# RG-LRU's squares in a tile of their own, and a new order of projection in the second half of a hybrid RWKV-7 / HGRN2 / RG-LRU layer

## The chip, the cores and the metric

The kernel runs on one core of a Trainium2 chip. The metric is the device time of one execution in microseconds (us), lower is better. The parts of the core that the text speaks of are TensorE (PE in the profile; its weight loads are listed as PEld), VectorE (DVE), ScalarE (ACT), GpSimd (POOL) and SyncE (SP). Each engine takes its own instructions strictly in order, and waits on semaphores for the others and for DMAs. SP issues the plain loads of weights; POOL issues the loads that accumulate.

## The reference

One layer of a recurrent decoder, all in fp32: 1024 prompt tokens and 8 sample tokens, 1032 columns in all, model width 1024.

```python
xn = rmsnorm(x, norm1_g)
pr, ph, pl = split(xn @ w_in)                    # 1408 + 1536 + 512 columns
pm = pr + mu_shift * (pr_previous_token - pr)
o_r = rwkv7(pm)     # 6 heads: S = S(diag(w) - kk^T (a kk)) + v^T k, per token
o_h = hgrn2(ph)     # 6 heads: S = diag(f) S + (1-f) i^T, o = S^T q, rmsnorm, gate
o_l = rglru(pl)     # 256 channels
x = x + concat(o_r, o_h, o_l) @ w_out
x = x + square(relu(rmsnorm(x) @ mlp_w1)) @ mlp_w2
y = rmsnorm(x)
...
def rglru(pl):
    xb, gate = split(pl)
    xc = conv_b + sum(xpad[:, j:j+T] * conv_w[j] for j in range(4))
    r, i = sigmoid(xc @ wa + ba), sigmoid(xc @ wx + bx)
    log_a = -8 * r * softplus(-lam)
    h = scan(exp(log_a), xc * i * sqrt(-expm1(2 * log_a)))
    return h * gelu(gate)
```

The gelu is the tanh form: it needs the square of the gate, gate * (1 + 0.044715 gate^2).

## The kernel before, in words

Channels lie on the 128 partitions, tokens along the free axis. The tokens go through the recurrent part in two halves, of 512 and of 520 columns. Heads are worked two at a time: RWKV has three pairs (r0, r1, r2 in the table `ORDER`), HGRN2 three (h0, h1, h2), RG-LRU two tiles of 128 channels (l0, l1); w is RWKV's low-rank part.

**Dense work.** A dense matmul in fp32 is done in three terms: weights and activations are split into a high part and a rest (`wh`, `wl`, `xh`, `xl`), and `dense_steps` issues wh*xh, wh*xl and wl*xh for each of 8 blocks of 128 rows, 24 matmuls for a tile of 128 output channels and one chunk of columns (the second half has chunks of 256 and 264 in the projections). `in_proj` does this for a tile of 128 columns of `w_in` (a pair of RWKV has 3 tiles, one of HGRN2 has 4: f, q, i, g; an LRU tile has 2: x and gate). `out_proj` does it for `w_out`, first for half 0 (out0_0 to out7_0, 512 columns each, called out0 to out7 below), then for half 1. It splits the finished columns of `mix` into `mh` (ACT, L1243) and `ml` (DVE, L1244), sums over the eight mix tiles in the order 0, 1, 3, 4, 6, 7, 2, 5, and then `evac` adds the residual (DVE, L1248), squares (ACT, L1254) and accumulates (DVE, L1255). After both come the two MLP products.

**Loads of weights.** `load_w` keeps one buffer for the raw weight and two each for `wh` and `wl`. SP loads the raw weight (L290), ACT rounds it to `wh` (L291). Then, for names in the table SOON, DVE subtracts (L293); for all others ACT writes -wh into `wl` (L295) and POOL issues a DMA that adds the raw weight to it (L296).

**Streams.** Beside the dense work run seven streams, written as generators: RWKV's chain (tiles `ch`, `mv`, `st`), two of its block inverses (`gram`, `xm`, `W`, `Y`), its operands (`pw` and others), its finish (`gate`), HGRN2 (`hg_run`: gram and state matmuls, then `ho`, a norm and the transposes `hoT`; in the second half `hg_sample` after it, with `hso` and `hsq`), and RG-LRU (`lru`). `weave` writes PE's order by hand: it keeps a clock `now` that every matmul advances by a cost from `mm` (L76 is where all matmuls are recorded), and takes the stream that is ready by estimated delays (`yield D23` and so on); the dense work fills what is left. The PE order is fixed by this; the other engines' instructions are ordered by the scheduler, with priorities.

**Buffers that hold the order back.** Projected tiles of HGRN2 and RG-LRU live in eight buffers with the tag `hpm`, those of RWKV in six with the tag `pm`. `take("hpm")` holds the dense work until a buffer is free by the planner's count `free["hpm"]`. A pair of HGRN2 takes four and gives them back at the end of `hg_run`; an LRU tile takes three: `xb`, `gl` (the gate) and `gq` (its square), and gives them back behind the last multiplication of `lru` (L1208). In `lru_proj` `gq` is filled as soon as a chunk of the gate leaves PSUM (ACT, L1142). In `lru` itself `gq` then becomes the argument of the tanh (L1158 to L1160), the gelu (L1161), and after the convolution (`lxc`, L1167 to L1172) the buffer of the input gate and of the multiplier of the scan.

The projection order of the second half is `w0 r0 h0 r1 h1 r2 h2 l0 l1`. The weights are loaded in the same order (`start`, the list `ahead`).

Of the kernel before, what the change touches and what calls it, by code (L numbers as in the profile page):

```python
# [9 lines left out]
F32 = mybir.dt.float32  # L10
F32R = mybir.dt.float32r
I32 = mybir.dt.int32
AF = mybir.ActivationFunctionType
# [4 lines left out]
P = 128  # L18
# [8 lines left out]
HW = HT + NB  # L27
# [13 lines left out]
SOON = tuple(f"in{col}_0" for col in (1152, 1280, 0, 384, 768, 2944, 3200, 1408, 1792, 2176, 2560)) + \  # L41
    ("out0_0", "out1_0") + tuple(f"out{m}_1" for m in range(8)) + tuple(f"w1_{f}" for f in range(4))
PRI = [-100, 0, 0, 300, 300, 300, 100, 300]
ORDER = [[(x[0], int(x[1])) for x in half.split()] for half in ("r0 w0 l0 h0 r1 l1 h1 r2 h2", "w0 r0 h0 r1 h1 r2 h2 l0 l1")]
NFB = FF // (FB * P)

COL_R, COL_K, COL_V, COL_WA, COL_G = 0, 384, 768, 1152, 1280
# [1 line left out]
COL_LX, COL_LG = 2944, 3200  # L49
# [3 lines left out]
def kernel(ctx: ExitStack, tc: tile.TileContext, i, o):  # L53
    nc = tc.nc
    V, S, G, PE = nc.vector, nc.scalar, nc.gpsimd, nc.tensor
    act = S.activation
# [37 lines left out]
    def bank_o(name):  # L94

        while now[0] < o_busy[0]:
            yield o_busy[0] - now[0]
        return ps("o", name)

    def used_o(delay=L_O):  # L100
        o_busy[0] = now[0] + delay

    def ev(key, delay=1.5):
        done[key] = now[0] + delay
# [91 lines left out]
    def vec(name, k, n=1):  # L196
        return vt[:, at[name] + k:at[name] + k + n]
# [123 lines left out]
    hgp = phase0.enter_context(tc.tile_pool(name="hgp", bufs=1, side="right"))  # L321
# [74 lines left out]
    free = {"pm": RPM, "hpm": HPM}  # L396

    def take(tag):

        yield lambda: free[tag] > 0  # L400
        free[tag] -= 1
# [8 lines left out]
    def next_w(ask=True):  # L410

        w = ahead.pop(0)()
        if ask:
            ask_w()
        return w


    rb0 = mix[dict(r=0, h=3, l=6)[ORDER[0][-1][0]] + ORDER[0][-1][1]][:, 0:HT]
    early = {}

    def project(hf, col, c0, n, bank="big"):

        pt = ps(bank, f"in{col}_{hf}_{c0}")
        yield from dense_steps(pt[:, :n], *ws_[0], lambda k: xh[k][:, c0:c0 + n], lambda k: xl[k][:, c0:c0 + n])
        return pt[:, :n]

    def take_out(hf, out, pt):

        if hf == 0:
            V.tensor_tensor(out, pt, rb0, op=ALU.mult)  # L430
        else:
            S.copy(out, pt)
# [3 lines left out]
    def in_proj(hf, col, evac, shift=False):  # L436

        if (hf, col) not in early:
            ws_[0] = next_w()
        for c0, n in HCH[hf]:  # L440
            if shift and c0 + n == HW:
                n += NB
            pt = early.pop((hf, col), None)
            if pt is None:
                pt = yield from project(hf, col, c0, n)
            if hf == 0 and ("rb",) not in done:
                yield ("rb",)
            evac(pt, c0, n)
# [439 lines left out]
    hgin, lruin = {}, {}  # L888

    def hp_tile(name):  # L890
        return hgp.tile([P, HW + 3], F32, tag="hpm", name=name, bufs=HPM)
# [237 lines left out]
    def lru_proj(t, hf):  # L1129
        if hf == 1:  # L1130
            yield ("LRU", t, 0)
        x = []
        for w in ("xb", "gl", "gq"):
            yield from take("hpm")
            x.append(hp_tile(f"l{w}{t}_{hf}"))
        xb, gl, gq = x
        G.tensor_copy(xb[:, 0:3], lcar[:, t, 0:3])
        yield from in_proj(hf, COL_LX + t * P, lambda pt, c0, n: take_out(hf, xb[:, 3 + c0:3 + c0 + n], pt))

        def evac_g(pt, c0, n):  # L1140
            take_out(hf, gl[:, c0:c0 + n], pt)
            act(gq[:, c0:c0 + n], gl[:, c0:c0 + n], AF.Square)  # L1142

        yield from in_proj(hf, COL_LG + t * P, evac_g)
        lruin[t, hf] = x
        ev(("lru", t, hf), 1.5)

    def lru(t, hf):
        yield ("lru", t, hf)
        xb, gl, gq = lruin[t, hf]  # L1150
        n = HT if hf == 0 else HW
        s0 = hf * HT

        def f(ap):
            return ap[:, 0:n]


        V.tensor_scalar(f(gq), f(gq), 0.044715, 1.0, op0=ALU.mult, op1=ALU.add)  # L1158
        V.tensor_tensor(f(gq), f(gq), f(gl), op=ALU.mult)
        act(f(gq), f(gq), AF.Tanh, scale=math.sqrt(2.0 / math.pi))  # L1160
        V.scalar_tensor_tensor(f(gl), f(gq), 1.0, f(gl), op0=ALU.add, op1=ALU.mult)  # L1161

        def cw(j):
            return vec("cw", 2 * j + t)

        xc = hgp.tile([P, HW], F32, tag="xc", name=f"lxc{t}_{hf}", bufs=1)
        V.tensor_scalar(f(xc), xb[:, 3:3 + n], cw(3), vec("cb", t), op0=ALU.mult, op1=ALU.add)  # L1167
        cv = cst[:, t, 0:24].rearrange("p (b j) -> p b j", j=3)
        for j in range(3):
            V.scalar_tensor_tensor(xc[:, 0:HT], xb[:, j:j + HT], cw(j), xc[:, 0:HT], op0=ALU.mult, op1=ALU.add)  # L1170
            if hf == 1:
                V.scalar_tensor_tensor(xc[:, HT:HW], cv[:, :, j], cw(j), xc[:, HT:HW], op0=ALU.mult, op1=ALU.add)  # L1172
        if hf == 0:
            V.tensor_copy(lcar[:, t, 0:3], xb[:, HT:HT + 3])
        else:

            so = small.tile([P, 36], F32, tag="lso", name=f"lso{t}", bufs=1)
            V.tensor_copy(so[:, 9:12], xb[:, HT:HT + 3])
            sv = so[:, 12:36].rearrange("p (b j) -> p b j", j=3)
            V.tensor_copy(sv[:, :, 0:2], cv[:, :, 1:3])  # L1180
            V.tensor_copy(sv[:, :, 2], xb[:, 3 + HT:3 + HW])
        rt, it = xb, gq
        yield D39
        for g, (dst, bias) in enumerate(((rt, hba), (it, hbx))):
            for c0, w in (((0, 512),) if hf == 0 else ((0, 260), (260, 260))):
                pt = yield from bank_o(f"lg{t}_{g}_{hf}_{c0}")
                mm(pt[:, 0:w], lruw[:, 2 * g + t, :], xc[:, c0:c0 + w])
                used_o()
                act(dst[:, c0:c0 + w], pt[:, 0:w], AF.Tanh, bias=bias[:, t:t + 1], scale=0.5)
                yield D40  # L1190

        V.scalar_tensor_tensor(f(xc), f(it), 1.0, f(xc), op0=ALU.add, op1=ALU.mult)
        m = gq
        act(f(m), f(rt), AF.Exp, bias=nsp2[:, t:t + 1], scale=nsp2[:, t:t + 1])
        act(f(rt), f(rt), AF.Tanh, bias=sp2[:, t:t + 1], scale=sp2[:, t:t + 1])
        V.scalar_tensor_tensor(f(m), f(m), 1.0, f(rt), op0=ALU.add, op1=ALU.mult)
        V.tensor_scalar(f(rt), f(m), -1.0, 1.0, op0=ALU.mult, op1=ALU.add)

        V.scalar_tensor_tensor(f(m), f(rt), 1.0, f(m), op0=ALU.add, op1=ALU.mult)
        V.tensor_scalar(f(m), f(m), 1e-12, None, op0=ALU.max)  # L1200
        act(f(m), f(m), AF.Sqrt)
        V.scalar_tensor_tensor(f(m), f(m), 0.5, f(xc), op0=ALU.mult, op1=ALU.mult)
        hs = xc
        V.tensor_tensor_scan(hs[:, 0:HT], rt[:, 0:HT], m[:, 0:HT], 0.0 if hf == 0 else lcar[:, t, 3:4], op0=ALU.mult, op1=ALU.add)
        if hf == 1:
            V.tensor_tensor(hs[:, HT:HW], rt[:, HT:HW], cst[:, t, 24:32], op=ALU.mult)
            V.tensor_tensor(hs[:, HT:HW], hs[:, HT:HW], m[:, HT:HW], op=ALU.add)
        V.scalar_tensor_tensor(mix[6 + t][:, s0:s0 + n], f(gl), 0.5, f(hs), op0=ALU.mult, op1=ALU.mult)  # L1208
        free["hpm"] += 3
        ev(("LRU", t, hf), 14.0)  # L1210
        if hf == 0:
            V.tensor_copy(lcar[:, t, 3:4], hs[:, HT - 1:HT])
            return
        V.tensor_copy(so[:, 0:9], hs[:, HT - 1:HW])
        nc.gpsimd.dma_start(o["lru"][t], so)
# [113 lines left out]
    def cols(group, j):  # L1329

        return [c + j * P for c in dict(w=(COL_WA, COL_G), r=(COL_R, COL_K, COL_V), h=(COL_HF, COL_HQ, COL_HI, COL_HG),
                                        l=(COL_LX, COL_LG))[group]]

    def projections():
        for col, bank in zip((col for group, j in ORDER[0] for col in cols(group, j)), ("big", "big", "o")):
            ws_[0] = next_w()
            early[0, col] = yield from project(0, col, 0, HT, bank)
        for hf in range(2):
            for group, j in ORDER[hf]:
                yield from dict(w=rw_lora, r=rw_proj, h=hg_proj, l=lru_proj)[group](j, hf)  # L1340
# [34 lines left out]
    def start():  # L1375

        ahead.extend((lambda col=col, hf=hf: load_w(i["w_in"][col // P], f"in{col}_{hf}", parts=2 if not hf and col == COL_WA else 1))
                     for hf in range(2) for group, j in ORDER[hf] for col in cols(group, j))
        ahead.extend((lambda m=m, hf=hf: load_w(i["w_out"][m], f"out{m}_{hf}")) for hf in range(2) for m in range(KT))
# [128 lines left out]
    for m in range(KT):  # L1508
        if m < 6:
            tag = ("wh8", "wl8", "raw8", "wl8", "wh8", "last")[m]  # L1510
            w = (mlp if m == 5 else wpool).tile([P, 2, FB, P], F32R, tag=tag, name=f"w2_{m}", bufs=2 if tag[0] == "w" else 1)
# [94 lines left out]
```

## Time and profile before

| | |
|---|---|
| time, median of three runs | 1594.58 us (1592.06 to 1597.8) |
| profiled execution, own time | 1598.09 us |
| its span | 1596.3 us |
| mean granted TensorE clock | 0.973 of full speed |
| PE busy | 1501.6 us, 94% of the span |
| PE weight loads busy | 1323.8 us, 83% |
| DVE busy | 770.7 us, 48% |
| ACT busy | 664.2 us, 42% |
| POOL busy | 382.8 us, 24% |

The own time of an execution is a little longer than its span, which runs from the first to the last recorded instruction. The second half's projections run from about 330 us on, the part that the change reorders lies between about 466 and 791 us, and from 791 us to the end there is only dense work (the rest of out_proj, then the MLP). In the views below, a row of the table by stretches of time gives the length of the stretch, then the busy time of PE, PEld, DVE, ACT and POOL with the number of instructions in brackets, the mean granted clock, the share of the DMA engines and GB/s. A row of the timeline gives start, duration, engine, line, operation and tiles, and in square brackets the wait ahead of it with the one that ended it.

### The profile page before, as it was taken

How to read it: one execution, taken by the hardware profiler on the slowest of the kernel's cores; microseconds unless marked ns; L12 is line 12 of the kernel's file. 1: busy time of each engine (PE TensorE's matmuls, PEld its weight loads, DVE VectorE, ACT ScalarE, POOL GpSimd, SP SyncE). 2: the span in 40 equal slices, each digit the busy share in tenths (PEclk: the TensorE clock that was granted, in tenths of full speed). 3: DMA queues.
4: the chain of work that ended last, by engine and by line, in shares of the span. 5: the costliest groups of instructions: out<-in, count | busy, mean ns of one | idle time of the engine just before them, and what ended most of it. 6: DMA issues, size and time to landing. Idle time of an engine off the chain costs nothing.

```text
span 1596.3 us, 30293 instructions
## 1 busy us (share of the span) xinstructions
PE 1501.6 (94%) x12536; PEld 1323.8 (83%) x12536; DVE 770.7 (48%) x1799; ACT 664.2 (42%) x1435; POOL 382.8 (24%) x531
## 2 busy tenths in 40 slices
PE   8879998998998989888899999999999999999997
PEld 6767776898997888777698989998989998989887
DVE  7778756766466657764465322222222222322224
ACT  4544656546346454454344423233232423233132
POOL 4553224225235245232222010101111010111011
PEclk9999999999899999978899999999999999999999
DMA  4325334334233344204533453535454454544242
GB/s 160 115 68 107 80 76 93 72 81 112 61 82 90 71 103 100 55 29 114 139 110 103 106 92 82 106 80 106 80 106 80 99 100 90 96 88 98 53 94 107
DMA packets 53081, 146.89 MB, mean 92 GB/s; under 512 B 6960, under 2 KB 7248, under 8 KB 52944
## 3 DMA queue, kind: packets, MB, share of 16 engines
q0 software_dynamic: 22976, 65.33, 24.7%
q1 hardware_dynamic: 29824, 79.61, 15.5%
q8 instruction: 98, 1.61, 0.4%
q14 instruction: 39, 0.32, 0.1%
q10 hardware_dynamic: 144, 0.04, 0.0%
HBM read 138.87 MB, written 6.07 MB: 91 GB/s over the span
## 4 chain that ended last, share of the span: by engine, by line
PE 45%; issue 5%; DMA 4%; DVE 3%; ACT 2%; POOL 1%; POOLq 0%; ACTq 0%; DVEq 0%
PE up L76 21%; PE dn L76 20%; PE out L76 2%; DMA raw_out<-in_w_out 1%; DMA wl_out<-in_w_out 1%; DMA wl_w<-in_w 1%; DMA raw_w<-in_w 1%; PE ch L76 1%; ACT wh_out L291 1%; PE in L76 1%; DVE wl_out L293 0%; PE fin L81 0%; DMA w<-in_w 0%; DVE ml L1244 0%; ACT wh_w L291 0%
## 5 line engine op out<-in xcount | busy, mean ns | idle before, releaser
L76 PE MATMUL in<-xl,wh_in 128*128 128x512 f32 (+3 forms) x648 | 222.2, 343 | 1.9 <-DVE xl L385 1.9
L76 PE MATMUL in<-xh,wl_in 128*128 128x512 f32 (+3 forms) x648 | 220.6, 340 | 3.4 <-DMA wl_in<-in_w_in 1.9
L76 PE MATMUL dn<-hh,wl_w 128*128 128x264 f32 (+2 forms) x696 | 222.9, 320 | 0.7 <-DMA wl_w<-in_w 0.6
L76 PE MATMUL dn<-hh,wh_w 128*128 128x264 f32 (+2 forms) x696 | 223.0, 320 | 0.0
L76 PE MATMUL dn<-hl,wh_w 128*128 128x264 f32 (+2 forms) x696 | 222.9, 320 | 0.0
L76 PE MATMUL in<-xh,wh_in 128*128 128x512 f32 (+3 forms) x648 | 221.7, 342 | 0.0
L1494 DVE TENSOR_TENSOR mix<-mix,dn 128x512 f32<-128x512 f32 (+2 forms) x192 | 98.3, 512 | 242.6 <-PE dn L76 242.6
L296 POOL DMA_DIRECT2D wl_w<-in_w x86 | 75.0, 875 | 574.4 <-ACT hh L1424 301.2
L291 ACT ACTIVATE wh_w<-raw_w 128x512 fp32r<-128x512 f32 (+1 forms) x90 | 70.6, 785 | 281.0 <-PE dn L76 228.2
L1423 DVE SCALAR_TENSOR_TENSOR rl<-up,rl 128x512 f32<-128x512 f32 (+2 forms) x96 | 49.5, 516 | 202.2 <-ACT rl L1422 202.2
L76 PE MATMUL up<-nxh,wh_w 128*128 128x264 f32 (+1 forms) x512 | 144.9, 283 | 0.1
L76 PE MATMUL up<-nxl,wh_w 128*128 128x264 f32 (+1 forms) x512 | 144.2, 282 | 0.5 <-POOL nxl L1320 0.5
L76 PE MATMUL up<-nxh,wl_w 128*128 128x264 f32 (+1 forms) x512 | 144.5, 282 | 0.0
L76 PEld LDWEIGHTS dn<-hh,wl_w 128*128 128x128 f32 x696 | 130.9, 188 | 13.6 <-DMA wl_w<-in_w 3.6
L76 PEld LDWEIGHTS dn<-hl,wh_w 128*128 128x128 f32 x696 | 131.0, 188 | 10.1
L76 PEld LDWEIGHTS dn<-hh,wh_w 128*128 128x128 f32 x696 | 131.1, 188 | 9.5
L76 PEld LDWEIGHTS in<-xl,wh_in 128*128 128x128 f32 x648 | 126.5, 195 | 14.6 <-DVE xl L385 4.6
L76 PEld LDWEIGHTS in<-xh,wl_in 128*128 128x128 f32 x648 | 126.3, 195 | 14.1 <-DMA wl_in<-in_w_in 2.4
L76 PEld LDWEIGHTS in<-xh,wh_in 128*128 128x128 f32 x648 | 126.3, 195 | 9.6 <-issue 0.2
L76 PE MATMUL up<-nh,wh_w 128*128 128x512 f32 x256 | 101.6, 397 | 0.0
L76 PE MATMUL up<-nl,wh_w 128*128 128x512 f32 x256 | 101.6, 397 | 0.0
L76 PE MATMUL up<-nh,wl_w 128*128 128x512 f32 x256 | 101.5, 397 | 0.0
(461 smaller groups left out, 3283.6 us busy)
## 6 DMA issues: line engine op xcount, KB each, us to landing
raw_in<-in_w_in SPq DMA_DIRECT2D x53, 512.0 KB, 3.3
wl_in<-in_w_in POOLq DMA_DIRECT2D x43, 512.0 KB, 5.5
raw_w<-in_w SPq DMA_DIRECT2D x32, 512.0 KB, 3.3
raw_w<-in_w SPq DMA_DIRECT2D x64, 256.0 KB, 2.6
wl_w<-in_w POOLq DMA_DIRECT2D x58, 256.0 KB, 4.1
wl_w<-in_w POOLq DMA_DIRECT2D x28, 512.0 KB, 5.5
raw_out<-in_w_out SPq DMA_DIRECT2D x16, 512.0 KB, 3.4
out_y_prompt<-yt SPq DMA_DIRECT2D x16, 256.0 KB, 2.0
```

The lines of the kernel that those rows point to most:

```text
L76: PE.matmul(out, lhsT, rhs, start=start, stop=stop)
L291: act(wh[:, ks], raw[:, ks], AF.Copy)
L296: G.dma_start(wl[:, ks], src[:, ks], accum_op=ALU.add)
L1423: V.scalar_tensor_tensor(rl[:, :n], pt[:, :n], 0.0, rl[:, :n], op0=ALU.max, op1=ALU.mult)
L1494: V.tensor_tensor(x2[m][:, c0:c0 + n], x2[m][:, c0:c0 + n], pt[:, :n], op=ALU.add)
```

## The change

Two things. First, `gq` no longer takes one of the eight shared `hpm` buffers. It is a tile of its own (tag `lq`, one buffer), which is requested when the LRU stream starts; the square moves with it, from two activations in `lru_proj` (one for each chunk of the second half) to one over the whole width in `lru`. An LRU tile so takes two `hpm` buffers and not three. Second, in the second half the projection order changes from `r1 h1 r2 h2` to `r1 r2 h1 h2`: RWKV's third pair is projected directly behind its second.

```diff
-ORDER = [[...] for half in ("r0 w0 l0 h0 r1 l1 h1 r2 h2", "w0 r0 h0 r1 h1 r2 h2 l0 l1")]
+ORDER = [[...] for half in ("r0 w0 l0 h0 r1 l1 h1 r2 h2", "w0 r0 h0 r1 r2 h1 h2 l0 l1")]
...
 def lru_proj(t, hf):
-        for w in ("xb", "gl", "gq"):
+        for w in ("xb", "gl"):
             yield from take("hpm")
             x.append(hp_tile(f"l{w}{t}_{hf}"))
-        xb, gl, gq = x
+        xb, gl = x
...
-        def evac_g(pt, c0, n):
-            take_out(hf, gl[:, c0:c0 + n], pt)
-            act(gq[:, c0:c0 + n], gl[:, c0:c0 + n], AF.Square)
-
-        yield from in_proj(hf, COL_LG + t * P, evac_g)
+        yield from in_proj(hf, COL_LG + t * P, lambda pt, c0, n: take_out(hf, gl[:, c0:c0 + n], pt))
...
 def lru(t, hf):
-        xb, gl, gq = lruin[t, hf]
+        xb, gl = lruin[t, hf]
+        gq = hgp.tile([P, HW], F32, tag="lq", name=f"lq{t}_{hf}", bufs=1)
...
+        act(f(gq), f(gl), AF.Square)
         V.tensor_scalar(f(gq), f(gq), 0.044715, 1.0, op0=ALU.mult, op1=ALU.add)
...
-        free["hpm"] += 3
+        free["hpm"] += 2
```

Every engine's order is the same as before through the whole first half, up to row 1724 of PE (466 us in the trace), and again from PE's row 3059 (the second chunk of half 1's out_proj, 791 us). Only what lies between is reordered. On SP the raw loads of r2's three weights move ahead of those of h1's four, on POOL the accumulating DMAs likewise. On PE the last `gram5` of HGRN2's second pair moves from row 2209 to 2430 and its `hsq` from 2437 to 2555; the first `pw` of RWKV's third pair moves from 2257 to 2039 and its last `gate` from 2998 to 2977. Names in the rows below: `in3200_1_256` is the projection of column 3200 of `w_in`, second half, chunk at 256; 2944 and 3200 are x and gate of l0, 3072 and 3328 those of l1.

PE at the end of l0's projection, before:

```order
L76 MATMUL in3200_1_256_8092<-xh7_3192,wh_in3200_1_7685 128x264
L76 MATMUL in3200_1_256_8092<-xl7_3200,wh_in3200_1_7685 128x264
L76 MATMUL in3200_1_256_8092<-xh7_3192,wl_in3200_1_7686 128x264
L76 MATMUL gram4_2_1_8186<-rq0_196,kq4_2_1_8126 64x2x32 x8
L76 MATMUL W3_2_1_1_8213<-xm_2_1_1_7880,sa_2_1_1_7878 64x64 x8
L76 MATMUL ch_2_1_0_8079<-st0_2_1_0_8167,az_186 128x64
L76 MATMUL Y3_2_1_1_8226<-ym_2_1_1_7879,wm3_2_1_1_8212 64x64 x8
L76 MATMUL ch_2_1_0_8079<-rh1_2_1_0_8224,yz_187 128x64
L76 MATMUL gram5_2_1_8239<-rq1_197,kq5_2_1_8179 64x2x32 x8
```

The same place now:

```order
L76 MATMUL in3200_1_256_8099<-xh7_3192,wh_in3200_1_7961 128x264
L76 MATMUL s_mean2_8146<-s_os2_7953,bones_84 128x8
L76 MATMUL in3200_1_256_8099<-xl7_3200,wh_in3200_1_7961 128x264
L76 MATMUL in3200_1_256_8099<-xh7_3192,wl_in3200_1_7962 128x264
L76 MATMUL in3072_1_0_8163<-xh0_3185,wh_in3072_1_8057 128x256
L76 MATMUL in3072_1_0_8163<-xl0_3193,wh_in3072_1_8057 128x256
L76 MATMUL in3072_1_0_8163<-xh0_3185,wl_in3072_1_8058 128x256
```

Before, 37 rows of stream matmuls (the third HGRN2 pair's `gram`, the inverse's `W` and `Y`, the chain's `ch`) stand between l0's last matmul and l1's first; now none does.

DVE at the end of LRU tile 0 (its last multiplication writes mix6) and the beginning of LRU tile 1 (`lq1`, `lxc1`), now; `mix1<-out1` is the residual addition behind out1:

```order
L728 COPY mv_2_1_1_7469<-ch_2_1_1_8374 128x64
L1205 TENSOR_TENSOR lxc0_1_8185<-lxc0_1_8185,lq0_1_8179 128x8
L1246 TENSOR_TENSOR mix1_70<-out1_0_8614,xr1_0_8612 128x512
L1206 SCALAR_TENSOR_TENSOR mix6_75<-lgl0_1_7958,lxc0_1_8185 128x520
L1212 COPY lso0_8193<-lxc0_1_8185 128x9
L1156 TENSOR_SCALAR lq1_1_8544<-lq1_1_8544 128x520
L1165 TENSOR_SCALAR lxc1_1_8550<-lxb1_1_8153,vt_77 128x520
L1157 TENSOR_TENSOR lq1_1_8544<-lq1_1_8544,lgl1_1_8154 128x520
L1253 TENSOR_TENSOR acc0_8453<-acc0_8453,sq1_0_8662 128x512
```

Before, mix6 stood nine rows ahead of the first operation on lxc1, among operations of the chain and the finish, with no addition of an out tile ahead of either. Now the addition behind out1 stands ahead of mix6, and the second LRU tile's operations follow it directly.

PE at the first gate matmul of LRU tile 1 (`lg1_0_1_0`, which reads lxc1), before:

```order
L76 MATMUL out1_0_8789<-mh7_8683,wl_out1_0_8776 128x512
L76 MATMUL ch_2_1_1_8588<-st1_2_1_1_8767,az_186 128x64
L76 MATMUL out1_0_8789<-mh2_8678,wh_out1_0_8775 128x512
L76 MATMUL out1_0_8789<-ml2_8686,wh_out1_0_8775 128x512
L76 MATMUL lg1_0_1_0_8813<-lxc1_1_8725,lruw_204 128x260
L76 MATMUL out1_0_8789<-mh2_8678,wl_out1_0_8776 128x512
```

And now:

```order
L76 MATMUL out1_0_8614<-ml5_8467,wh_out1_0_8600 128x512
L76 MATMUL out1_0_8614<-mh5_8459,wl_out1_0_8601 128x512
L76 MATMUL out2_0_8674<-mh0_8454,wh_out2_0_8606 128x512
L76 MATMUL out2_0_8674<-ml0_8462,wh_out2_0_8606 128x512
L76 MATMUL lg1_0_1_0_8677<-lxc1_1_8550,lruw_204 128x260
L76 MATMUL ch_2_1_1_8374<-mv_2_1_1_7469,bt_2_1_1_7222 128x64
```

The gate matmul has moved from inside out1 to three rows behind out1's last.

More of the change, by code (lines that the diff above doesn't have):

```diff
@@ L43 @@
 PRI = [-100, 0, 0, 300, 300, 300, 100, 300]
-ORDER = [[(x[0], int(x[1])) for x in half.split()] for half in ("r0 w0 l0 h0 r1 l1 h1 r2 h2", "w0 r0 h0 r1 h1 r2 h2 l0 l1")]
+ORDER = [[(x[0], int(x[1])) for x in half.split()] for half in ("r0 w0 l0 h0 r1 l1 h1 r2 h2", "w0 r0 h0 r1 r2 h1 h2 l0 l1")]
 NFB = FF // (FB * P)
```

## The prediction

> **What bounds the kernel now.** I read the first part of the page for the share of each engine, then the chain of waits by engine, then the table by stretches of time.
>
> ```profile
> PE 1501.6 (94%) x12536; PEld 1323.8 (83%) x12536; DVE 770.7 (48%) x1799; ACT 664.2 (42%) x1435; POOL 382.8 (24%) x531
> PE 45%; issue 5%; DMA 4%; DVE 3%; ACT 2%; POOL 1%; POOLq 0%; ACTq 0%; DVEq 0%
> ```
>
> PE is busy for 94% of the span and leads the chain; no other engine reaches 50%. So a change that leaves PE's work alone can only win where PE idles or where its clock is low. The five stretches show where that is:
>
> ```profile
> 466.00:669.00 203.00, 186.78 (x2432) 168.96 (x2434) 134.54 (x391) 103.26 (x284) 82.85 (x114) 0.99 0.36 83
> 669.00:691.00 22.00, 19.16 (x252) 15.61 (x253) 11.59 (x33) 9.41 (x22) 5.15 (x10) 0.61 0.21 49
> 691.00:737.00 46.00, 37.67 (x261) 32.49 (x261) 25.99 (x63) 21.21 (x59) 13.30 (x16) 0.81 0.20 55
> 737.00:791.00 54.00, 45.34 (x235) 36.14 (x234) 25.47 (x48) 27.56 (x50) 11.59 (x17) 0.94 0.60 151
> 791.00:1596.00 805.00, 786.51 (x5078) 712.38 (x5078) 253.81 (x491) 259.51 (x464) 106.03 (x125) 1.00 0.44 94
> ```
>
> From 466 to 669 us and from 791 us on PE is full at full clock. Between lie 122 us of two defects: PE busy 82 to 87%, and a clock of 0.61, 0.81 and 0.94. The first of the three begins where the dense work stops and ends where it starts again:
>
> ```profile
> 668.68 0.28 PE L76 MATMUL in<-xh,wl_in 128*128 128x264 f32 x1
> 668.89 0.69 PE L76 MATMUL gram<-rq,kq 128*64 128x64 f32 x16
> ...
> 685.45 1.23 PE L76 MATMUL lg<-lxc,lruw 128*128 128x260 f32 x2
> ...
> 690.77 0.36 PE L76 MATMUL in<-xh,wh_in 128*128 128x256 f32 x1
> ```
>
> The last matmul of l0's projection starts at 668.68, the first of l1's at 690.77. This is the hole in front.md's first pair of order rows: h1 and h2 hold all eight `hpm` buffers, and when h1's four come back l0 takes three, so l1 must wait. In the hole only stream matmuls are left, and they run slowly: the pair of `lg` at 685.45 takes 1.23 us, the same pair inside out_proj 0.60 (row below). The clock is what differs:
>
> ```profile
> 680.00:690.00 10.00, 10.00 (x136) 8.06 (x136) 4.47 (x13) 4.30 (x10) 1.73 (x4) 0.50 0.01 3
> 739.18 0.60 PE L76 MATMUL lg<-lxc,lruw 128*128 128x260 f32 x2
> ```
>
> PE counts as busy for 10.00 of 10 us there, at a clock of 0.50, so it does 5 us of work. Busy time times clock gives the work at full clock: 19.16 x 0.61 = 11.7 us, 37.67 x 0.81 = 30.5, 45.34 x 0.94 = 42.6, together 84.8 us in 122 us.
>
> **The change part by part.**
>
> *The hole is filled.* With two buffers for an LRU tile, h1's four serve l0 and l1, and l1's projection follows l0's without a stream row between. The third RWKV pair's chain starts earlier too (its first `pw` moves from PE row 2257 to 2039, the last `gate` from 2998 to 2977), so that the streams run beside dense work and not alone. PE's work is the same. The full stretch (466 to 669) does 186.78 x 0.99 / 203 = 0.91 us of work in each us. At that rate the three stretches need 11.7 / 0.91 = 12.8, 30.5 / 0.91 = 33.5 and 42.6 / 0.91 = 46.8 us: they lose 9.2, 12.5 and 7.2 us, 28.9 in all. I take the first two, 21.7, and leave the 7.2 where they are, since out2 to out7 wait there for weights, whose loading isn't changed:
>
> ```profile
> PE out L76 <- DMA wl_out<-in_w_out: 8.1, 4, 4.4
> PE gate L76 <- DVE mix L782: 2.9, 1, 2.9
> PE hsq L76 <- DVE hssq L1115: 2.2, 1, 2.2
> ```
>
> The first row's 8.1 us are four waits of PE between 690 and 792. The waits for `gate` and `hsq` are of the size that the 9% of the full stretch already holds.
>
> *The end of LRU tile 0 in front of tile 1.* This adds a wait. By front.md's last order rows DVE now has the addition behind out1 (mix1) ahead of mix6, and everything for the second LRU tile behind that; and PE has `lg1_0_1_0`, which needs the finished lxc1, three rows behind out1's last matmul. So from out1's end PE does two matmuls and then waits for a string of DVE instructions. Their groups, each with busy time and mean ns:
>
> ```profile
> L1248 DVE TENSOR_TENSOR mix<-out,xr 128x512 f32<-128x512 f32 x8 | 5.5, 690 | 9.1 <-PE out L76 9.1
> L1255 DVE TENSOR_TENSOR acc<-acc,sq 128x512 f32<-128x512 f32 x7 | 4.8, 688 | 2.7 <-ACT sq L1254 2.7
> L1170 DVE SCALAR_TENSOR_TENSOR lxc<-lxb,vt,lxc 128x512 f32<-128x512 f32 x6 | 4.5, 744 | 0.0
> L1172 DVE SCALAR_TENSOR_TENSOR lxc<-lcst,vt,lxc 128x8 f32<-128x8 f32 x6 | 2.9, 480 | 0.0
> L1159 DVE TENSOR_TENSOR lgq<-lgq,lgl 128x520 f32<-128x520 f32 x2 | 1.4, 696 | 0.0
> L1208 DVE SCALAR_TENSOR_TENSOR mix<-lgl,lxc 128x520 f32<-128x520 f32 x2 | 1.4, 694 | 0.0
> L1161 DVE SCALAR_TENSOR_TENSOR lgl<-lgq,lgl 128x520 f32<-128x520 f32 x2 | 1.4, 680 | 1.8 <-ACT lgq L1160 1.8
> L1167 DVE TENSOR_SCALAR lxc<-lxb,vt 128x520 f32<-128x520 f32 x2 | 1.1, 547 | 0.6 <-ACT lxb L432 0.6
> L1158 DVE TENSOR_SCALAR lgq<-lgq 128x520 f32<-128x520 f32 x2 | 0.9, 427 | 0.7 <-ACT lgq L1142 0.7
> L1178 DVE COPY lso<-lxb 128x3 f32<-128x3 f32 x2 | 0.4, 210 | 0.0
> ```
>
> 0.69 (mix1) + 0.69 (mix6) + 0.43 + 0.55 + 0.70 + 0.69 (acc) + 3 x 0.74 (convolution) + 0.68 (gelu) = 6.7 us. With three of L1172 and four copies it is 6.7 + 7 x 0.21 (L1178's) = 8.1 to 6.7 + 3 x 0.48 + 4 x 0.21 = 9.0. I take the lower end, since one of the six L1172 is far longer than the rest, and take 0.6 for the two matmuls in front: 7.5 us of waiting. Queued behind it on PE are out2 to out7, all dense. A wait of this size also costs clock. The nearest row is a wait of 4.39 us for a weight, with the 10 us around it:
>
> ```profile
> 765.53 0.73 PE L76 MATMUL out<-mh,wl_out 128*128 128x512 f32 x1 [4.39 <-DMA wl_out<-in_w_out]
> 760.00:770.00 10.00, 5.61 (x20) 4.20 (x20) 3.08 (x8) 2.52 (x3) 3.03 (x5) 0.83 0.84 183
> ```
>
> A clock of 0.83 over 10 us loses 1.7 us. Together 9.2 us; at least 0, if out2's weight is what PE would wait for in that time anyway (the 8.1 above are then paid at once).
>
> The Trainium skill, page "TensorE: Matmul & The Clock Gate", Part 1, says that the clock halves after an idle window of about 3.4 us and is full again after about 3.4 us of sustained work. This trace agrees in the size behind the 4.39 us wait, but not in the hole, where PE is busy for 10.00 of 10 us at 0.50. By the rule the `hoT` wait below, past 3.4 us as well, would cost 1.7 us more, and the sum would be a gain of 6.3 us and not 8.0.
>
> *HGRN's second pair moves back.* With r2 projected first, h1's matmuls come later and its tail is squeezed: 125 PE rows from the second pair's last `gram5` to its `hsq`, where there were 228. The step from `ho` to `hoT` is the tight one:
>
> ```profile
> 590.47 1.72 PE L76 MATMUL ho<-hst,rq 128*64 128x64 f32 x32
> 603.35 0.66 PE L81 MATMUL hoT<-ident,hot 128*128 128x128 f32 x4 [2.23 <-DVE hot L1083]
> 572.34 0.69 PE L76 MATMUL gram<-rq,kq 128*64 128x64 f32 x16
> 616.34 0.28 PE L76 MATMUL hsq<-hssq,bones 128*128 128x8 f32 x2
> ```
>
> From 592.2 to 603.35 pass 11.2 us, 2.2 of them idle. In the new order fewer rows stand between: I estimate 3 us more of waiting (between 0 and the 9 that are covered now), and 1.5 for `hso` and `hsq`: 4.5 us.
>
> *The square.* One activation over 520 columns in place of two over 256 and 264, on ACT, which is under half busy. For tile 0 dense work covers it. For tile 1 its buffer comes free ahead of mix1, so it runs while DVE waits for out1: nothing. Without that cover it delays L1158 by its own length, which no row shows at this width; DVE's operations on 520 columns take 0.43 to 0.70 us.
>
> *Loads.* On SP three raw loads of r2, on POOL their accumulating DMAs, pass four of h1, in the order in which PE uses them: nothing. If the cover failed, the price is that of the waits for projection weights now:
>
> ```profile
> PE in L76 <- DMA wl_in<-in_w_in: 1.9, 2, 1.6
> ```
>
> **The sum.** 21.7 - 9.2 - 4.5 = 8.0 us gained. The profiled execution took 1598.1 us, 3.5 above the median of the runs: 1590.1 against it, 1586.6, or 1587, against the median of 1594.58. Bounds: with `lg1`'s clock and HGRN's waits at nothing the gain is 8.0 + 1.7 + 4.5 = 14.2 (1580); with half of the second stretch's 12.5 not recovered, 1.7 (1593).
>
> **The rivals.**
>
> *All of the hole, no new wait.* If DVE has mix1's place early enough, or out2's weight is late anyway, and `hoT` is covered, the gain is 21.7 to 28.9 us: 1566 to 1573. For it: DVE is 48% busy, and the scheduler has let such waits vanish in most places of the full stretch. Against it: the string is in DVE's order, and it can't begin before out1's end. Chance 0.20.
>
> *HGRN's tail is a latency, not a matter of rows (slower).* From `gram5` to `hsq` the second pair took 616.34 - 572.34 = 44.0 us over 228 rows, 0.193 us a row. 125 rows now give 24 us. If the tail needs the 44 whatever stands beside it (DVE, ACT and POOL between), PE waits 20 us in place of the 4.5: 15.5 us more, a loss of 7.5, 1602. It decides against the change from 4.5 + 8.0 = 12.5 us of idle PE in that stretch on. For it: the waits for `hoT` are there even with 228 rows. Against it: the waits for `hoT` and `hsq` are 2.2 us each at most, so much of the 44 us is PE's own queue. Chance 0.17.
>
> *The clock does not come back.* If the small matmuls themselves pull the clock down, the hole's 19.16 us of busy time stay 19.16, not 11.7: the gain shrinks by 7.5 to 0.5 us, 1594. Against it: the same small matmuls run between dense ones at 0.99 from 466 to 669 us. Chance 0.08.
>
> That the change doesn't do what it says is ruled out by the order: l1's first row follows l0's last.
>
> **How the numbers follow.** My forecast has 0.55. A measurement of this kernel can tell 0.3%, 4.8 us. Of the forecast's own range, 1580 to 1593, three quarters lie below 1589.8: 0.41, and 0.14 within. With the first rival faster has 0.61. Same: 0.14 + 0.08 + 0.03 of the second rival, 0.25. Slower: the 0.14 left. The range reaches to 1570, two fifths into the first rival's, and to 1602, the middle of the second's: some 0.12 lies below and 0.08 above.
>
> **What would show it.** In the new profile: no stretch of over 5 us without a dense matmul between 466 and 740 us, and no clock of 0.5 to 0.6 there over 10 us (right), or one (the third rival). A wait of PE `lg` for DVE `lxc` of about 7 us behind out1, with the clock down after it; if it is under 2, the first rival. The waits of `hoT`, `hso` and `hsq` for the second pair summing to about 4.5 us above now; 12 or more and the second rival has it. The waits for `wl_out` at about 8 us as now; if they grow, a loss that I have not priced. The prediction is wrong if the time from PE's row 1724 to row 3059, 325 us now, is not 311 to 323 (the bounds of the sum).

## The result, and the profile after

The changed kernel takes 1580.78 us (median of 20 runs, 1572.17 to 1590.88) against 1594.51 us before (20 runs, 1591.04 to 1602.88): the ratio is 0.9912, 95% interval 0.9895 to 0.9929, a gain of 13.7 us where 7.5 were forecast (1587 against 1594.58). The profiled execution of the changed kernel took 1572.8 us, 8.0 below its median, and that of before 1598.09, 3.5 above. So the two traces differ by 25 us, more than the kernels do, and 3 of the 25 lie ahead of the first moved row (466.08 us before, 463.04 now), where the two programs are the same.

The page after, first the busy times, then the chain of waits by engine:

```profile
PE 1489.7 (95%) x12536; PEld 1312.6 (84%) x12536; DVE 771.2 (49%) x1799; ACT 663.7 (42%) x1433; POOL 382.8 (24%) x531
PE 74%; DVE 11%; ACT 6%; DMA 4%; issue 4%; POOL 1%; POOLq 0%; SPq 0%; ACTq 0%; DVEq 0%
```

PE has the same 12536 matmuls and is 12 us less busy with them (1501.6 before): they are the same, the clock under them is higher. The stretches of time of the changed kernel show where; the reordered part now ends at 766.3 us and not at 791:

```profile
463.00:624.00 161.00, 152.46 (x1997) 139.57 (x1997) 104.61 (x304) 86.68 (x225) 61.17 (x89) 1.00 0.37 84
624.00:646.50 22.50, 18.15 (x299) 14.86 (x298) 13.26 (x41) 9.54 (x46) 11.28 (x16) 0.77 0.30 76
646.50:702.40 55.90, 54.04 (x492) 46.90 (x491) 42.74 (x107) 31.09 (x68) 19.86 (x26) 1.00 0.35 84
702.40:720.00 17.60, 10.79 (x56) 8.95 (x56) 9.06 (x24) 6.84 (x11) 2.69 (x5) 0.81 0.41 97
720.00:766.30 46.30, 41.20 (x337) 32.74 (x335) 27.30 (x58) 25.97 (x63) 17.96 (x21) 1.00 0.60 150
766.30:1571.00 804.70, 786.39 (x5078) 712.10 (x5078) 254.63 (x492) 259.77 (x464) 106.30 (x125) 0.99 0.44 94
```

Busy time times clock adds up to 270.4 us of work from 463 to 766.3, and before to 269.8 (185 + 84.8), so the method counts the same work in both traces. Before it took 325 us, now 303. Two rows stand out, 624 to 646.5 at a clock of 0.77 and 702.4 to 720 with PE busy 10.79 of 17.6 us. PE's timeline has the reasons:

```profile
624.01 0.28 PE L76 MATMUL in<-xh,wl_in 128*128 128x264 f32 x1
...
646.48 0.36 PE L76 MATMUL in<-xh,wh_in 128*128 128x256 f32 x1
...
663.24 0.29 PE L76 MATMUL in<-xh,wl_in 128*128 128x264 f32 x1
663.36 0.28 PE L76 MATMUL in<-xh,wh_in 128*128 128x256 f32 x1
...
709.24 0.80 PE L76 MATMUL lg<-lxc,lruw 128*128 128x260 f32 x1 [6.81 <-DVE lxc L1168]
```

At 663 us l1's projection follows l0's without a gap: the hole that the prediction spoke of is gone. But at 624 there is another, of 22.5 us, that it didn't speak of. Between the last matmul of h2's projection and the first of l0's PE has only stream matmuls. h1 and h2 hold all eight buffers, and the new order brings h1's pair later, so that now l0 and not l1 waits for its end. And at 702.4 begins the wait at `lg` that was forecast. PE's waits from 690 to 767 us, in total, number and longest:

```profile
PE lg L76 <- DVE lxc L1168: 6.8, 1, 6.8
PE ho L76 <- DVE hst L1060: 2.6, 3, 1.2
PE out L76 <- DMA wl_out<-in_w_out: 1.9, 2, 1.3
```

The waits for `wl_out` went from 8.1 us to 1.9. On DVE, the string that ends the wait at `lg`:

```profile
702.29 0.69 DVE L1246 TENSOR_TENSOR mix<-out,xr 128x512 f32<-128x512 f32 x1
702.89 0.69 DVE L1206 SCALAR_TENSOR_TENSOR mix<-lgl,lxc 128x520 f32<-128x520 f32 x1
...
709.10 0.22 DVE L1170 SCALAR_TENSOR_TENSOR lxc<-lcst,vt,lxc 128x8 f32<-128x8 f32 x1
```

From mix1 at 702.29 to the end of lxc1's last operation pass 7.0 us, where the prediction summed 8.1 at the lower end. And mix1 shows no wait ahead of it: DVE came to it as out1 ended (the last matmul ends at 702.44), with work behind work since 688 us.

### The profile page after: what moved, and what is told of

The parts are those of the page before. It is cut to its first block, busy times and chain, and to the rows that moved or that the text cites. A ratio compares the mean times of both kernels' runs of the same rounds, so it can differ in the third digit from the quotient of the medians.

```text
span 1571.0 us, 30303 instructions
## 1 busy us (share of the span) xinstructions
PE 1489.7 (95%) x12536; PEld 1312.6 (84%) x12536; DVE 771.2 (49%) x1799; ACT 663.7 (42%) x1433; POOL 382.8 (24%) x531
## 4 chain that ended last, share of the span: by engine, by line
PE 74%; DVE 11%; ACT 6%; DMA 4%; issue 4%; POOL 1%; POOLq 0%; SPq 0%; ACTq 0%; DVEq 0%
PE up L76 22%; PE dn L76 21%; PE in L76 14%; PE ch L76 3%; PE W L76 2%; PE out L76 2%; PE Y L76 2%; PE gram L76 1%; DMA raw_out<-in_w_out 1%; PE sc L76 1%; DMA raw_w<-in_w 1%; ACT wh_out L291 1%; DMA raw_in<-in_w_in 1%; DVE rq L981 1%; DMA wl_w<-in_w 1%
## 5 line engine op out<-in xcount | busy, mean ns | idle before, releaser
L76 PEld LDWEIGHTS in<-xh,wl_in 128*128 128x128 f32 x648 | 124.7, 192 | 11.7 <-DVE wl_in L293 1.9
L1420 ACT ACTIVATE rl<-up 128x512 f32<-128x512 f32 (+2 forms) x96 | 43.3, 451 | 139.5 <-PE up L76 139.5
```

The source lines that it names most:

```text
L76: PE.matmul(out, lhsT, rhs, start=start, stop=stop)
L1420: act(rl[:, :n], pt[:, :n], AF.Relu)
```

## The experiments

The theory after the result: the gain is the filled hole, and the wait at `lg` and the new hole take part of it back. Two rivals: that the gain comes from the third RWKV pair's earlier chain, and that the waits are paid once, whatever ends them. All times are medians, all ratios are to the kernel before, timed beside the experiment.

**Half of the change: the buffers alone.**

```diff
-... "w0 r0 h0 r1 r2 h1 h2 l0 l1"
+... "w0 r0 h0 r1 h1 r2 h2 l0 l1"
```

> The squares in their own tile and two shared buffers for an LRU tile, with the old projection order (r1 h1 r2 h2). In PE's order l1's projection then follows l0's directly, as in the changed kernel; RWKV's third pair is projected as late as before. Theory A (the gain is the hole in the dense work, and only the buffers close it): nearly the whole gain, 8 to 16 us below the kernel before, and no stretch at clock 0.5 between l0 and l1. Theory B (the gain is that the third RWKV pair's chain starts earlier and ends earlier): within 4 us of the kernel before, since its last gate still comes at PE row 3064.

Measured: 1576.91 us, ratio 0.9900 (0.9874 to 0.9926). The same stretch of time as the hole of before, then the rest of the reordered part:

```profile
669.00:691.00 22.00, 22.00 (x296) 20.18 (x296) 12.75 (x30) 11.25 (x25) 5.18 (x9) 1.00 0.31 73
691.00:776.00 85.00, 73.05 (x472) 59.96 (x472) 51.75 (x117) 46.75 (x105) 25.95 (x34) 0.90 0.50 123
```

From 669 to 691 us PE is busy all the time at full clock, where before it did 11.7 us of work. The buffers alone give as much as the whole change or more (the intervals overlap): theory A holds. The profiled execution was the slowest of the six (1582.58 us).

**The other half: the order alone.**

```diff
-        for w in ("xb", "gl"):
+        for w in ("xb", "gl", "gq"):
```

(and the square back in `lru_proj`.)

> The new projection order with three shared buffers for an LRU tile, as before the change. In PE's order 45 rows of stream matmuls stand again between l0's projection and l1's. Theory A (the hole): 0 to 5 us from the kernel before, with a stretch of some 15 to 20 us at a clock of about 0.5. Theory B (the third RWKV pair earlier): 8 to 16 us below the kernel before.

Measured: 1589.97 us, ratio 0.9979 (0.9961 to 0.9997). The hole ahead of l1 is back, 23 us, and so is the clock of one half:

```profile
664.00:687.00 23.00, 17.80 (x142) 13.74 (x140) 14.92 (x41) 11.55 (x36) 6.62 (x9) 0.63 0.21 46
670.00:680.00 10.00, 8.49 (x67) 6.63 (x63) 6.63 (x16) 4.67 (x22) 1.85 (x2) 0.50 0.25 48
```

The order alone gains some 3 to 6 us (by the ratio and by the medians) with both holes in it, l0's and l1's. So the buffers carry the gain, but the order is not worth nothing.

**The waiting matmul moved.** The gate matmuls of LRU tile 1 come later on PE, behind out2's end; nothing else changes.

```diff
-        yield D39
+        yield D39 + (8 if (t, hf) == (1, 1) else 0)
```

> The changed kernel with 8 us more of estimated delay ahead of LRU tile 1's gate matmuls, so that the first of them stands at PE row 2892 and not 2860, behind out2. Theory A (the wait for lxc1 is a loss by itself): the wait of 6.8 us behind out1 is gone, and with it the lower clock: 6 to 9 us below the changed kernel, about 1572 to 1575. Rival (out2 and out3 wait for their weights in that time anyway, so the wait is paid once whatever ends it): waits for wl_out grow by 4 to 6 us and the time is within 3 us of the changed kernel.

Measured: 1567.41 us, ratio 0.9839 (0.9810 to 0.9868). The changed kernel, timed beside it (below), took 1585.38; a gain of 6 to 9 us on it was expected. PE's largest wait from 690 to 767 us, then the two stretches in which the changed kernel waited:

```profile
PE out L76 <- DMA wl_out<-in_w_out: 5.1, 5, 2.0
```

```profile
700.00:710.00 10.00, 8.97 (x55) 7.13 (x54) 9.10 (x24) 5.40 (x7) 2.87 (x5) 1.00 0.80 180
710.00:720.00 10.00, 9.09 (x113) 7.43 (x112) 3.92 (x13) 7.04 (x25) 2.23 (x3) 1.00 0.58 137
```

The wait is gone, and the waits for weights grow from 1.9 to 5.1, so the rival has some 3 us. From out2's first matmul to the end of the reordered part (766.3 us in the first profile of the changed kernel) pass 57.1 us here, and 64.4, 69.1 and 66.3 us in the three profiles of the changed kernel. The wait at `lg` so cost 7 to 12 us, about the 9.2 of the prediction. By the medians of the two kernels, timed together, it cost 18 us, which is more than the profiles show. This version is faster than both kernels by far.

**The changed kernel again, twice.**

> The changed kernel itself once more, for a second profile: its 20 runs lie between 1572 and 1591 us, and the profiled one was 8 us below their median. If the spread comes from the clock, this profile shows the same waits as the first (lg behind out1 about 6.8 us) and low-clock stretches at other places; if it comes from waits, these differ by several us. The median should be 1578 to 1584.

> The changed kernel a third time. Its two profiles have the same waits of PE to within 1 us, but 5.1 us between them, in the stretch from 730 to 760 us, where one has a granted clock of 1.00 and the other 0.66, 0.96 and 0.87 over three times 10 us. Theory (the spread of this kernel's runs is where and how long the clock stays low behind its waits and behind the hole ahead of l0): again lg about 6.8 us, the hole from 624 to 646 us, and a median of 1579 to 1587. Rival: other waits than in the first two profiles.

Measured: 1585.38 us (12 runs), ratio 0.9939 (0.9917 to 0.9960), and 1582.56 (6 runs), 0.9911 (0.9889 to 0.9933); the first median is just above the 1578 to 1584 that were expected. The wait at `lg` is 6.8 us all three times. What differs is the clock; the same stretch in the first, second and third profile of the changed kernel:

```profile
730.00:740.00 10.00, 8.56 (x50) 6.97 (x49) 6.79 (x21) 4.30 (x19) 7.58 (x9) 1.00 0.34 109
```

```profile
730.00:740.00 10.00, 7.59 (x32) 5.96 (x32) 5.76 (x18) 4.38 (x25) 6.06 (x7) 0.66 0.15 37
```

```profile
730.00:740.00 10.00, 9.36 (x39) 7.55 (x40) 5.09 (x18) 4.40 (x19) 6.63 (x8) 0.67 0.31 85
```

Over all 38 runs the median is 1582.2 us. The fastest 12 average 1577.8 us at a mean clock of 0.979, the slowest 12 average 1587.8 at 0.974. A clock lower by 0.005 over 1580 us would be 8 us of those 10. But a run that waits longer also has a lower mean clock, so the lists alone don't show which comes first. Between the first two profiles it is the clock: their waits are the same to within about 1 us, and from 730 to 760 us the mean clock is 1.00 in the first and 0.83 in the second, which is worth about the 5.1 us between them. All three profiled executions lie well below the medians that go with them (1572.8, 1577.91 and 1577.26 us), so no trace shows what an execution of 1585 us does. That it loses its time by the clock too is likely, and not shown; at which places stays open.

**The wait's buffer.** LRU tile 1's lxc gets a buffer that tile 0 doesn't hold, so that DVE can fill it early; PE's order stays.

```diff
-        xc = hgp.tile([P, HW], F32, tag="xc", name=f"lxc{t}_{hf}", bufs=1)
+        xc = hgp.tile([P, HW], F32, tag="xc" if (t, hf) != (1, 1) else "kq", name=f"lxc{t}_{hf}", bufs=1 if (t, hf) != (1, 1) else 2)
```

> The changed kernel with LRU tile 1's convolution result lxc1 in another buffer (one of the two that HGRN2 uses for kq), so that it need not wait until tile 0 is done with the one xc buffer; PE's order is unchanged, and DVE's puts all of lxc1's operations some 20 rows ahead of the addition behind out1. Theory A (PE waits at lg1 for the end of a string of DVE work that the one buffer ties to tile 0's end): the wait of 6.8 us behind out1 falls below 2 us with PE's order as it is, and the time is 6 to 12 us below the changed kernel, 1570 to 1576. Rival (DVE is full in that stretch, whatever its order): the work moved ahead delays the ml splits and HGRN's operations by as much, new waits of 4 to 7 us stand at gram, ho or out, and the time is within 4 us of the changed kernel.

Measured: 1585.64 us, ratio 0.9911 (0.9883 to 0.9938), so no gain. Rows of PE, ACT and DVE:

```profile
720.48 1.24 PE L76 MATMUL lg<-lxc,lruw 128*128 128x260 f32 x2 [5.29 <-ACT lxb L1187]
```

```profile
719.95 0.48 ACT L1187 ACTIVATE lxb<-lg,hba 128x260 f32<-128x260 f32 x1 [2.45 <-DVE lso L1179]
```

```profile
719.54 0.17 DVE L1176 COPY lso<-lxb 128x3 f32<-128x3 f32 x1 [1.31 <-DMA out_lru<-lso]
```

The first gate matmul no longer waits (it starts at 710.13). But the third waits 5.29 us, for ACT to empty its bank into `lxb`. ACT waits for DVE's copies of `lxb` into `lso`, and these for tile 0's output DMA, since `lso` too has one buffer. The wait went to the next buffer that the two tiles share. The rival's result holds, though the new wait is not at `gram`, `ho` or `out`, where it was expected, and at its end a DMA is waited for, not DVE's work (DVE is idle for the last 1.31 us ahead of the copies). The clock took more as well, in the hole ahead of l0:

```profile
640.00:650.00 10.00, 9.16 (x87) 6.89 (x83) 4.32 (x13) 0.78 (x3) 4.06 (x6) 0.50 0.07 28
650.00:660.00 10.00, 10.00 (x62) 9.71 (x62) 4.23 (x15) 0.48 (x2) 5.07 (x6) 0.54 0.08 26
```

Here the clock stays at half for 9.4 us after the dense matmuls have come back (at 649.9). In the changed kernel's first profile, with the same order on PE, it was full again 4.9 us before they came back (at 646.48). First this run, then the changed kernel's first profile:

```profile
649.90:659.30 9.40, 9.40 (x57) 9.11 (x58) 4.23 (x15) 0.58 (x2) 4.61 (x5) 0.50 0.08 28
```

```profile
631.40:641.60 10.20, 8.68 (x89) 6.64 (x87) 3.87 (x12) 3.33 (x18) 4.32 (x5) 0.50 0.20 56
641.60:646.50 4.90, 3.72 (x75) 3.08 (x75) 3.20 (x10) 0.30 (x2) 3.56 (x5) 1.00 0.15 57
```

So PE's order alone does not fix how long the clock stays down; what does is open.

**Idle matmuls in the old hole.** In the kernel before, 86 matmuls (128x256) of l0's last weight, whose result nobody reads, go into the hole ahead of l1.

```diff
+        if (t, hf) == (1, 1):
+            pt = ps("big", "fill")
+            while free["hpm"] < 3:
+                mm(pt[:, 0:256], ws_[0][0][:, 0, :], xh[0][:, 0:256])
+                yield 0.0
```

> The kernel before with 86 idle matmuls (128x256, l0's last weight times xh, never read) put into the hole between l0's and l1's projection, wherever the planner has nothing else there. They are some 10 us of work at full clock. Theory A (the clock halves there because PE has only small matmuls to do, and dense ones bring it back): the hole keeps its length of about 22 us or grows by up to 3, with a clock near 1.0, and the time is within 4 us of the kernel before in spite of the 10 us of work. Rival (the small matmuls themselves take that long): the hole grows by 10 us at the least, and the time with it.

Measured: 1599.27 us, ratio 1.0018 (1.0003 to 1.0033). The hole, a pair of `lg` in it, its first filling and the first matmul behind it:

```profile
667.50:690.50 23.00, 23.00 (x339) 20.97 (x337) 11.58 (x33) 8.55 (x18) 2.95 (x7) 1.00 0.03 10
```

```profile
667.54 1.20 PE L76 MATMUL fill<-xh,wh_in 128*128 128x256 f32 x9
...
683.73 0.60 PE L76 MATMUL lg<-lxc,lruw 128*128 128x260 f32 x2
...
690.50 0.36 PE L76 MATMUL in<-xh,wh_in 128*128 128x256 f32 x1
```

The hole takes 23.0 us instead of 21.9, with ten more of work in it. The `lg` pair takes 0.60 us and not 1.23, and the clock is 1.00 and not 0.50. So the clock is what made the hole's own matmuls slow, and with dense matmuls between them it stays up. This settles the prediction's third rival: the small matmuls are not slow by themselves.

**The new hole filled.** In the changed kernel l0 is projected ahead of h2.

```diff
-... "w0 r0 h0 r1 r2 h1 h2 l0 l1"
+... "w0 r0 h0 r1 r2 h1 l0 h2 l1"
```

> The changed kernel with one more step in the projection order: l0 ahead of h2 (r1 r2 h1 l0 h2 l1). In the changed kernel's trace PE has no dense matmul from 624.0 to 646.5 us, since l0 waits there for the buffers of HGRN2's second pair; by the order of this kernel no such hole is left, and LRU tile 0 ends long before tile 1's gate matmuls. Theory A (a second hole, opened by the new order, and the wait at lg1 are what the change leaves on the table): no clock of 0.5 to 0.6 over 10 us, no wait of over 2 us at lg, 12 to 18 us below the changed kernel, 1565 to 1570. Rival (the streams' own chains set the end of half 0's out_proj): the third HGRN2 pair's tail comes later (its hsq at PE row 3058), new waits take the place, and the time is within 5 us of the changed kernel.

Measured: 1570.67 us (4 runs), ratio 0.9835 (0.9817 to 0.9853), with 1.3 us of waiting at `lg` and no stretch of over 6.5 us without a dense matmul. That is as fast as with the waiting matmul moved (1567.41, 0.9839), and that version still has the hole ahead of l0:

```profile
624.00:646.50 22.50, 18.14 (x299) 14.88 (x298) 13.16 (x41) 9.52 (x45) 11.14 (x16) 0.77 0.29 76
```

So the wait at `lg` is shown to cost time, but that anything is won by filling the hole as well is not: either the hole costs less than its clock suggests, or moving l0 costs as much elsewhere, and no run tells the two apart.

**A wait added.** In the version with the buffers alone, LRU tile 1's gate matmuls come 6 us earlier, where lxc1 isn't ready.

```diff
-        yield D39
+        yield D39 - (6 if (t, hf) == (1, 1) else 0)
```

> The wait at lg put into a kernel that has none: the run with the new buffers and the old projection order (1576.9 us), with 6 us less of estimated delay ahead of LRU tile 1's gate matmuls. The first of them moves from PE row 2859 to 2833, some 6 us of dense matmuls earlier, while in the trace of that kernel lxc1 is ready only 0.3 us before PE asks for it. Theory A (a wait at lg costs its own length and clock behind it, whatever the projection order): a wait of 4 to 7 us at lg, and a time 6 to 14 us above, 1583 to 1591. Rival (it is paid once, since out2 and out3 wait for their weights anyway): waits for wl_out shrink by as much as lg waits, and the time is within 3 us of 1576.9.

Measured: 1585.21 us, ratio 0.9926 (0.9906 to 0.9946), 8.3 us above the version without the wait by the medians, which were not timed together, and 4 by the ratios; the two intervals overlap, so the sign is likely and the size not sure. PE's two largest waits from 690 to 780 us, and the largest in the version without:

```profile
PE out L76 <- DMA wl_out<-in_w_out: 6.0, 3, 2.5
PE lg L76 <- DVE lxc L1168: 5.4, 1, 5.4
```

```profile
PE out L76 <- DMA wl_out<-in_w_out: 6.6, 3, 3.4
```

The wait at `lg` is 5.4 us, and the waits for weights hardly shrink: by the profiles it is not paid once.

**The same two holes filled with the old order.** As the run before the last, but with r2 behind h1.

```diff
-... "w0 r0 h0 r1 r2 h1 l0 h2 l1"
+... "w0 r0 h0 r1 h1 r2 l0 h2 l1"
```

> The run with the new buffers and the old order, with l0 ahead of h2 (r1 h1 r2 l0 h2 l1). By the order there is no hole without dense matmuls, and LRU tile 0 ends long before tile 1's gates. Theory A (PE's free time is all that is left to win, and the third RWKV pair's late chain costs little): 1566 to 1573, as fast as with r2 ahead of h1. Rival (r2's chain, which here runs through half 0's out_proj, breaks up the dense work there and keeps the clock down): no faster than 1576.9 by more than 2 us.

Measured: 1584.02 us, ratio 0.9920 (0.9899 to 0.9941); theory A's 1566 to 1573 are missed. PE from the point at which the two orders part (with r2's or h1's first matmul) to out1's end, first with r2 ahead of h1, then with r2 behind, and PE's two largest waits of the latter from 460 to 830 us:

```profile
465.90:704.60 238.70, 220.29 (x2748) 198.13 (x2747) 160.12 (x452) 130.39 (x341) 90.46 (x128) 1.00 0.36 84
```

```profile
463.20:713.70 250.50, 228.95 (x2790) 204.40 (x2790) 164.09 (x460) 132.16 (x343) 91.62 (x127) 0.98 0.35 81
PE ch L76 <- DVE st L737: 4.6, 6, 1.4
PE ch L76 <- DVE rh L724: 4.3, 3, 2.6
```

Without a long hole (8.9 us at most here) and without a wait of over 1.3 us at `lg` on either side, r2 ahead of h1 is worth 13.4 us by the medians (1570.67 against 1584.02), of which 11.8 show up to out1's end. Where they come from is shown only in part. PE waits for r2's chain (`ch`) in both: 10.2 us in all here, and 6.5 with r2 ahead of h1, where this is the largest row of waits in the same stretch:

```profile
PE ch L76 <- DVE st L737: 5.9, 6, 2.1
```

The 13.4 us also hold only with l0 ahead of h2 on both sides. The buffers alone (1576.91 us), without a long hole or a wait at `lg` either, lie 6.2 us above the one and 7.1 us below the other, though not timed with them. So the order has a worth of its own, 6 to 13 us by what it is set against, that the change's own hole and wait had hidden, and l0 ahead of h2 does not pay with the old order.

## Why the prediction was right, point by point

The direction, the range (1570 to 1602) and the leading mechanism held; the range is wide and has the time before in it too. The gain was 13.7 us and not 7.5, near the upper bound of 14.2. The test that the prediction set itself, 311 to 323 us from row 1724 to row 3059, was missed on the fast side by all three profiles (303.2, 307.8 and 305.4). So the sum was too small, and that the median still lies inside its bounds is partly luck: the three profiled executions are 5 to 8 us faster than their medians.

The prediction's first sign misled. A stretch without dense matmuls and a clock of 0.5 to 0.6 over 10 us was to speak for the third rival. There is one (0.50 from 631.4 to 641.6 us), but it lies in the new hole ahead of l0, which the prediction did not have, and not in the one that it asked about.

*The hole is filled (21.7 us).* Right, and shown by the two halves of the change and by the idle matmuls. With the buffers alone the clock there comes back to 1.00.

*The wait at lg (9.2 us).* Right in place and size: 6.8 us of waiting, forecast 7.5; the whole price is 7 to 12 us by the profiles. One point is open: the string was said to begin at out1's end, but DVE was working without a pause and reached mix1 as out1 ended (702.29 against 702.44), so this trace can't tell which of the two set its start. The tie is the buffers that the two LRU tiles share, and freeing one shows the next.

*HGRN's second pair (4.5 us of waiting).* Wrong in kind. The rows between `gram5` and `hsq` were counted, 125 where 228 had stood, but not looked at: the last of them, from 624.2 us to l0's first at 646.48, have no dense matmul among them. The waits for `hoT`, `hso` and `hsq` there are small:

```profile
PE hoT L81 <- ACT wm L672: 1.2, 1, 1.2
```

The price is that of a hole, about half of it idle time of PE (4.35 us, in waits of at most 1.2 us for `hoT`, `ch`, `gate` and `W`) and half of it clock. From 624 to 646.5 us 18.15 x 0.77 = 14.0 us of work are done; at the 0.911 of the prediction they take 15.4, so 7.1 us are lost in the first profile. No run shows that they can be won (the run with l0 ahead of h2).

*out2 to out7 keep their 7.2 us.* Wrong in the first profile: the stretch from 720 us on does 41.2 us of work in 46.3, which loses 1.1 at the same rate, and the waits for `wl_out` fell from 8.1 to 1.9. Part of that is the wait at `lg`, during which weights arrive (5.1 without it). In the second and third profile the same rows take 50.9 us at a clock of 0.90 and 48.4 at 0.93, and lose some 6 and 3 us, now by the clock and not for weights.

*The order costs nothing but HGRN's waits.* This is the largest of the steps that made the sum too small. From 463 to 624 us PE does 152.46 us of work in 161, 0.947 in each us against the 0.911 taken; that is 6.4 us. From 646.5 to 702.4 it does 0.967, another 3.4. The prediction took the rate of the old full stretch for a ceiling. The first of the two comes from the order: the order alone has it, the buffers alone don't (152.35 x 1.00 and 147.62 x 0.98 in the same 161 us, first the order alone):

```profile
463.40:624.40 161.00, 152.35 (x1997) 139.46 (x1997) 104.62 (x304) 86.61 (x225) 60.48 (x89) 1.00 0.37 84
```

```profile
465.90:626.90 161.00, 147.62 (x1846) 134.40 (x1846) 100.88 (x298) 83.72 (x229) 72.19 (x99) 0.98 0.39 89
```

Together: 8.0 + 6.4 + 3.4 (rates) + 6.1 (out2 to out7) - 2.6 (HGRN 7.1 for 4.5) + 1.2 (`lg`, 8.0 in this trace) = 22.5, and the trace shows 21.6 in the reordered part. The terms come from the same rows as the time, so this checks the adding up and is no second proof. The medians show 13.7: the profiled execution lies 8.0 us below its own.

*The rivals.* That no new wait appears fell with the 6.8 us at `lg`. That HGRN's tail is a latency was half right: from `gram5` to `hsq` the second pair now takes 34.6 us (611.62 to 646.23), between the 24 of the rows and the 44 of before, but PE idles only 4.35 us of the hole, under the 12.5 from which it would have decided. That the clock does not come back fell with the idle matmuls.

## What to carry to other kernels

When an order of work is changed, look in the new order for every place where the filling work stops, not only at the one that the change is to close: such a place moves to whoever now waits for the same buffers. Here a wait of PE for a chain went away when the waiting instruction was moved behind other work, and not when one of several buffers that tie the chain was freed. Try the parts of a change alone and in pairs: here each part alone had a gain, and the wait at `lg`, which only the two together have, took part of it back.

## What the runs showed of the hardware

The granted clock can fall to 0.50 while PE is busy for 10.00 of 10 us with small matmuls (680 to 690 us before), and it is 1.00 in the same place with dense ones between (the idle matmuls). It need not stay down with small ones: in the new hole it was 1.00 from 641.6 to 646.5 us. The Trainium skill, page "TensorE: Matmul & The Clock Gate", Part 1, says that the gate looks at how busy PE has been; these runs show that the busy time of the profile is not that measure. The same part says that its window runs freely, so that the time to full clock varies from run to run of one kernel. The runs agree that it varies: around the end of the hole ahead of l0 the clock was full from 641.6 us on in one execution, and 0.50 up to 659.3 us in another with the same order on PE, with PE busy on dense matmuls for the last 9.40 of 9.40 us. That is longer than the 3.4 us of sustained work that the prediction quotes from the Trainium skill, and no run here shows the reason. The 38 runs of one program spread over 19 us.
